# Top-16 searches run as two interleaved chains, and the index decode in two passes instead of three

## The chip, the cores and the metric

The kernel runs on one core of a Trainium2 chip. The metric is the device time of one execution in microseconds (us). A core has these engines, each with its own in-order instruction queue: TensorE (PE in the profile; PEld is its weight loads), VectorE (DVE), ScalarE (ACT), GpSimd (POOL) and SyncE (SP, here only issuing transfers). They meet at semaphores.

## The reference

One step of a hybrid decoder layer for 256 prompt tokens and 8 sample tokens (264 columns, `T`). What matters here is the PEER block: for every token and each of 8 heads, two score vectors of 128 keys are searched for their 16 largest, the 16x16 sums are searched again, and the winners name 16 of 16384 experts.

```python
s1 = jnp.einsum('thd,hkd->thk', q[:, :, 0], keys1)
s2 = jnp.einsum('thd,hkd->thk', q[:, :, 1], keys2)
t1, i1 = lax.top_k(s1, 16)
t2, i2 = lax.top_k(s2, 16)
cand = t1[..., :, None] + t2[..., None, :]          # 16 x 16 per head
cand_idx = i1[..., :, None] * 128 + i2[..., None, :]
top, pos = lax.top_k(cand.reshape(..., 256), 16)
idx = jnp.take_along_axis(cand_idx, pos, axis=-1)
gate = jax.nn.softmax(top, axis=-1)
hid = gelu(einsum('td,thkd->thk', x, u_tab[idx]))
out = einsum('thk,thkd->td', gate * hid, v_tab[idx])
```

## The kernel before

All matrix products are made in three (or, paired, two) passes over a weight split into a high and a low part. For each half of a 128-column weight block (1 MB block, halves of 128x1024) ScalarE writes the high part, `whi` (line 165, a cast), and VectorE writes the low part, `wlo` (line 166, a subtraction). `split_w` does it as soon as a buffer pair is free; there are 4 pairs, 5 from the PEER stage on. So VectorE stands in every half of every matrix product of the program: the PE cannot enter the `wlo` products of a half before line 166 has run for it.

The program is written out in one stream by hand. `pair_block` and `col_block` write the products of one half and then call `tick(budget)`. A tick lets background generators (`tasks`) write some of their instructions between this half and the next: each `yield c` of a generator takes c from the tick's budget of 1.1, and `yield ("w", n)` sleeps n ticks. The constants in the yields thus set how many background instructions stand between two `wlo` rows of VectorE's queue. A burst of them with no yield stands there whole.

The stretch in question:

- The query projection (`col_block` over `w_q`) and then the U stage: 128 blocks `pair_block(x1_p, u_evac(e), 1.1)`, which compute x times all experts' u rows densely. In each half 8 steps of one 416-column product (line 303) and one 208-column product (line 304), 16 steps in a block; the evacuation is one `as` copy on ScalarE (line 1452), one `as` addition on VectorE (line 1453), and a Gelu every second block (1456).
- Beside it, background work. `head_topk(h)` makes the scores of a head on the PE (`scr`, `scp`) and searches them with `topk` (lines 1111 to 1116): five VectorE operations, each needing the one ahead. The processor's form of `max_index` and `match_replace` is two instructions each, MATCH_VALUE_LOAD and FIND_INDEX8 or MATCH_REPLACE8.
- `select(t, sel)`: for t = 0 and 2 a grid of 128 tokens with 8 heads, for t = 1 a small one (64 rows, 1 head). It adds the candidates (`cand`, 112 per head), searches each head's (lines 1174 to 1178), works out the two slot numbers a and b of each winner from its position (nine small steps, 1183 to 1193), and decodes them into key indices: for each quarter of the heads and each side s, `big` = (a equals slot) (1205), times `idf`, the key indices as floats (1208), summed over slots (1210). Then the softmax, `sel`.
- `select_all` runs the grids in the order 0, 1, 2. Grid 0's result is transposed by the PE (`slt`, line 1240) into `slot`, and starts `gates`, which every three ticks makes one-hot tiles `o` of four tokens on POOL (line 1289, three of four; the fourth on VectorE) and ScalarE (1290), and multiplies them on the PE (`gps`, line 1302). Grid 1 starts `sparse_experts`, which fetches expert rows `ug` by indirect transfers that POOL issues (1313) and works on them on VectorE (1383). Grid 2 runs beside both.
- `iot` holds the numbers 0 to 127 in each partition; it is fetched by POOL's queue at the program's start.

Of the kernel before, what the change touches and what calls it, by code (L numbers as in the profile page):

```python
# [31 lines left out]
TOPK = 16  # L32
# [3 lines left out]
NEG = -3.0e38  # L36
# [16 lines left out]
def hybrid_step(ctx: ExitStack, tc: tile.TileContext, xT, pT, w_in, w_dt, w_bs, w_bc, w_o, w_q, w_pg, w_pp,  # L53
                uT, vP, uR, vR, keysT, par, hpar, hist, h0, eye, tri, iota, fold, yT, o_hp, o_hs, o_cp, o_cs, o_sp, o_ss):
    nc = tc.nc
    te, ve, ac, gp, sy = nc.tensor, nc.vector, nc.scalar, nc.gpsimd, nc.sync

    cpool = ctx.enter_context(tc.tile_pool(name="cpool", bufs=1))
# [53 lines left out]
    def bank(name):  # L112
        return BG["pool"].tile([128, 512], F, name=name, tag="bg", bufs=BG["n"])
# [979 lines left out]
    def load_keys(h):  # L1093
        k = t2.tile([128, 2, 128], F, name="keys", tag="keys", bufs=2)
        gp.dma_start(out=k, in_=keysT[:, 2 * h:2 * h + 2, :])
        keys_sb[h] = k
# [10 lines left out]
            defer(3, late)  # L1107
        return f

    def topk(v, a, i, n):  # L1110
        ve.max(a[:, 0:8], v)
        ve.max_index(i[:, 0:8], a[:, 0:8], v)
        w = t2.tile([128, 128], F, name="sw", tag="sw", bufs=2)
        ve.match_replace(w[:n], a[:, 0:8], v, NEG)
        ve.max(a[:, 8:16], w[:n])
        ve.max_index(i[:, 8:16], a[:, 8:16], w[:n])

    def head_topk(h):
        load_keys(h)
        yield ("w", 2)  # L1120
        for s in range(2):
            ac.copy(zq[:, s, h, 8 * h:8 * h + 8], Q[2 * h + s][:, PT:T])
        yield ("w", 1)
        k = keys_sb.pop(h)
        ps2 = {}
        for t in (0, 2):
            t0, n, _ = TT[t]
            ps = bank("scr")
            for s in range(2):
                te.matmul(ps[:n, s * 128:(s + 1) * 128], Q[2 * h + s][:, t0:t0 + n], k[:, s], start=True, stop=True)  # L1130
            v = t2.tile([128, 2, 128], F, name="sv", tag="sv", bufs=3)
            ac.copy(v[:n].rearrange("p s k -> p (s k)"), ps[:n, 0:256])
            ps2[t] = v
            yield 0.1
        if h == 0:
            SC["ps"] = bank("scp")
        for s in range(2):
            te.matmul(SC["ps"][:64, s * 128:(s + 1) * 128], zq[:, s, h], k[:, s],
                      start=(h == 0 and s == 0), stop=(h == PH - 1), skip_group_check=True)
        if h == PH - 1:  # L1140
            v = t2.tile([128, 2, 128], F, name="sv", tag="sv", bufs=3)
            ac.copy(v[:64].rearrange("p s k -> p (s k)"), SC.pop("ps")[:64, 0:256])
            ps2[1] = v
        for t, v in sorted(ps2.items()):
            n = TT[t][1]
            for s in range(2):
                hh = h if t != 1 else 0
                topk(v[:n, s], TV[t][s][:n, hh], TI[t][s][:n, hh], n)
                yield 1.1
        Q.pop(2 * h)  # L1150
        Q.pop(2 * h + 1)
        DONE[h] = True

    def select(t, sel):

        _, n, nh = TT[t]
        sp = P["sp"]
        w = nh * TOPK
        top = sp.tile([128, nh, TOPK], F, name="top", tag="top", bufs=1)
        pos_u = sp.tile([128, nh, TOPK], U32, name="posu", tag="posu", bufs=1)  # L1160

        cand = sp.tile([128, nh, 112], F, name="cand", tag="cand", bufs=1)
        v1, v2 = TV[t][0][:n], TV[t][1][:n]
        ve.tensor_tensor(cand[:n, :, 0:64].rearrange("p h (a b) -> p h a b", b=16),
                         v1[:, :, 0:4, None].to_broadcast([n, nh, 4, 16]),
                         v2[:, :, None, :].to_broadcast([n, nh, 4, 16]), OP.add)
        ve.tensor_tensor(cand[:n, :, 64:112].rearrange("p h (a b) -> p h a b", b=4),
                         v1[:, :, 4:16, None].to_broadcast([n, nh, 12, 4]),
                         v2[:, :, None, 0:4].to_broadcast([n, nh, 12, 4]), OP.add)
        yield 1.1  # L1170
        for h in range(nh):
            cf = cand[:n, h]
            a, i = top[:n, h], pos_u[:n, h]
            ve.max(a[:, 0:8], cf)
            ve.max_index(i[:, 0:8], a[:, 0:8], cf)
            ve.match_replace(cf, a[:, 0:8], cf, NEG)
            ve.max(a[:, 8:16], cf)
            ve.max_index(i[:, 8:16], a[:, 8:16], cf)
# [3 lines left out]
        sh = sp.tile([128, w], U32, name="sh", tag="sh", bufs=2)
        ve.tensor_scalar(sh[:n], pu, 4, None, OP.logical_shift_right)
        ve.tensor_copy(ab_f[:n, 2], sh[:n])
        sh = sp.tile([128, w], U32, name="sh", tag="sh", bufs=2)
        ve.tensor_scalar(sh[:n], pu, 2, None, OP.logical_shift_right)
        ve.tensor_copy(ab_f[:n, 3], sh[:n])
        fa, fb = ab_f[:n, 0], ab_f[:n, 1]
        ve.scalar_tensor_tensor(fa, ab_f[:n, 3], -12.0, ab_f[:n, 2], OP.add, OP.max)
        ve.tensor_scalar(ab_f[:n, 2], fa, 4.0, 48.0, OP.mult, OP.add)  # L1190
        ve.scalar_tensor_tensor(ab_f[:n, 2], fa, 16.0, ab_f[:n, 2], OP.mult, OP.min)
        ve.tensor_copy(fb, pu)
        ve.tensor_tensor(fb, fb, ab_f[:n, 2], OP.subtract)
        yield 1.4
        HH = max(1, nh // 4)
        for s in range(2):
            af = ab_f[:, s].rearrange("p (h k) -> p h k", h=nh)
            idf = sp.tile([128, nh, TOPK], F, name="idf", tag="idf", bufs=1)
            ve.tensor_copy(idf[:n], TI[t][s][:n])
            sv = sel[:n, s].rearrange("p (h k) -> p h k", h=nh)  # L1200
            for h0_ in range(0, nh, HH):
                hs = slice(h0_, h0_ + HH)
                big = sp.tile([128, HH, TOPK, TOPK], F, name="big", tag="big", bufs=1)
                sh4 = [n, HH, TOPK, TOPK]
                ve.tensor_tensor(big[:n], af[:n, hs, :, None].to_broadcast(sh4),
                                 iot[:n, None, None, 0:TOPK].to_broadcast(sh4), OP.is_equal)
                yield 0.6 if nh > 1 else 0.4
                ve.tensor_tensor(big[:n], big[:n], idf[:n, hs, None, :].to_broadcast(sh4), OP.mult)
                yield 0.6 if nh > 1 else 0.4
                ve.tensor_reduce(sv[:, hs], big[:n], AX.X, OP.add)  # L1210
                yield 0.6 if nh > 1 else 0.4
        gt = sel[:n, 2].rearrange("p (h k) -> p h k", h=nh)
        ve.tensor_tensor(gt, top[:n], top[:n, :, 0:1].to_broadcast([n, nh, TOPK]), OP.subtract)
        yield ("w", 1)
        ac.activation(gt, gt, AF.Exp)
        sm = sp.tile([128, nh], F, name="sm", tag="sm", bufs=2)
        ve.tensor_reduce(sm[:n], gt, AX.X, OP.add)
        ve.reciprocal(sm[:n], sm[:n])
        ve.tensor_tensor(gt, gt, sm[:n, :, None].to_broadcast([n, nh, TOPK]), OP.mult)
        yield 0.8  # L1220
# [554 lines left out]
```

## Time and profile before

| what | value |
|---|---|
| runs shown | 2433.89, 2436.02, 2436.13 us, median 2436.02 |
| profiled execution | 2436.66 us, of which the span of the records is 2434.7 us |
| PE busy | 2410.7 us, 99% of the span |
| DVE busy | 2004.6 us, 82% |
| ACT busy | 1451.3 us, 60% |
| POOL busy | 664.9 us, 27% |
| DMA | 685.49 MB, mean 282 GB/s |

A table by stretches of time has, for each engine, the time it was busy and in brackets the number of instructions, then the granted PE clock (1.00 is full speed), the share of time that the DMA engines were busy, and GB/s. A line of the timeline has start, duration, engine, source line, operation, output<-inputs, shape, count, and in square brackets the idle time ahead of it and what ended it. A line of the waits has who waited for whom, the sum in us, how often, and the longest.

Line numbers from about 118 on move by a few lines in the changed kernel (166 becomes 167, 1453 becomes 1459).

### The profile page before, as it was taken

To read this page: it belongs to the slowest core of one execution; us is meant where nothing else is said; L and a number is where in the kernel's file an instruction comes from. 1 tells how busy PE (TensorE), PEld (TensorE's weight loads), DVE (VectorE), ACT (ScalarE), POOL (GpSimd) and SP (SyncE) were. 2 spreads that over 40 slices of the span, in tenths; PEclk is the share of its full clock that TensorE was granted. 3 is DMA by queue.
4 is the path that set the end of the run, shared out by engine and by line. 5 is a ranking of instruction groups with operands and counts; after the bars stand their busy time and mean duration, and the time that the engine had idled before them with its cause. 6 is when DMAs were issued, how large, how long until landed. Compare 5 with 4: busy or idle time off the path is not lost.

```text
span 2434.7 us, 47923 instructions
## 1 busy us (share of the span) xinstructions
PE 2410.7 (99%) x19049; PEld 2397.1 (98%) x19049; DVE 2004.6 (82%) x3178; ACT 1451.3 (60%) x2310; POOL 664.9 (27%) x716
## 2 busy tenths in 40 slices
PE   9999999999999999999999999999999999999999
PEld 9999999999999999999999999999999999999999
DVE  7788887567455578999989877789999999999997
ACT  6776664554444455754677878777554455444574
POOL 2232221000000010100149767663433233322210
PEclk9999999999999999999999999999999999999999
DMA  6697786555555555566779999999999999999553
GB/s 246 230 293 256 257 262 213 195 189 199 199 192 193 198 198 191 197 224 199 237 266 367 388 354 358 353 383 404 392 397 389 395 387 389 393 374 370 201 200 131
DMA packets 135632, 685.49 MB, mean 282 GB/s; under 512 B 15552, under 2 KB 51952, under 8 KB 61808
## 3 DMA queue, kind: packets, MB, share of 16 engines
q1 hardware_dynamic: 89168, 495.46, 56.8%
q0 software_dynamic: 28368, 156.99, 16.6%
q10 hardware_dynamic: 17872, 29.99, 3.4%
q8 instruction: 149, 2.44, 0.4%
q14 instruction: 75, 0.61, 0.1%
HBM read 644.61 MB, written 37.76 MB: 280 GB/s over the span
## 4 chain that ended last, share of the span: by engine, by line
PE 82%; DVE 11%; issue 2%; ACT 2%; DMA 2%; POOL 0%; ACTq 0%; DVEq 0%; SPq 0%; POOLq 0%
PE mm L303 21%; PE mm L264 14%; PE mm L266 14%; PE mm L265 14%; PE mm L304 11%; DVE wlo L166 5%; PE kept L303 2%; PE mm L306 1%; PE gps L1302 1%; PE kept L304 1%; ACT whi L165 1%; DMA a_d<-as 1%; DVE as L1453 1%; DMA ug<-vR,sidx 0%; DVE ug L1383 0%
## 5 line engine op out<-in xcount | busy, mean ns | idle before, releaser
L166 DVE TENSOR_TENSOR wlo<-w,whi 128x1024 fp32r<-128x1024 f32 x916 | 1112.6, 1224 | 282.9 <-ACT whi L165 274.2
L165 ACT CAST whi<-w 128x1024 fp32r<-128x1024 f32 x916 | 953.0, 1045 | 538.1 <-PE mm L265 192.7
L303 PE MATMUL mm<-x,whi 128*128 128x416 f32 x1920 | 571.5, 365 | 0.0
L264 PE MATMUL mm<-x,whi 128*128 128x264 f32 x1920 | 532.4, 277 | 0.0
L266 PE MATMUL mm<-x,wlo 128*128 128x264 f32 x1920 | 530.2, 276 | 1.1 <-DVE wlo L166 1.1
L265 PE MATMUL mm<-x,whi 128*128 128x264 f32 x1920 | 529.9, 276 | 0.0
L304 PE MATMUL mm<-x,wlo 128*128 128x208 f32 x2048 | 502.7, 256 | 7.8 <-DVE wlo L166 7.8
L303 PE MATMUL mm<-co,whi 128*128 128x416 f32 x1680 | 490.5, 361 | 0.0
L304 PE MATMUL mm<-co,wlo 128*128 128x208 f32 x1792 | 436.9, 254 | 0.0
L304 PEld LDWEIGHTS mm<-x,wlo 128*128 128x128 f32 x2048 | 393.2, 193 | 11.0 <-DVE wlo L166 10.9
L303 PEld LDWEIGHTS mm<-x,whi 128*128 128x128 f32 x1920 | 365.8, 191 | 1.2 <-issue 0.5
L266 PEld LDWEIGHTS mm<-x,wlo 128*128 128x128 f32 x1920 | 362.9, 189 | 1.7 <-DVE wlo L166 1.7
L264 PEld LDWEIGHTS mm<-x,whi 128*128 128x128 f32 x1920 | 362.9, 189 | 1.4 <-issue 1.4
L265 PEld LDWEIGHTS mm<-x,whi 128*128 128x128 f32 x1920 | 362.9, 189 | 0.0
L304 PEld LDWEIGHTS mm<-co,wlo 128*128 128x128 f32 x1792 | 341.9, 192 | 0.0
L303 PEld LDWEIGHTS mm<-co,whi 128*128 128x128 f32 x1680 | 317.9, 189 | 0.0
L1289 POOL TENSOR_SCALAR o<-iot,slot,slot 128x128 f32<-128x128 f32 x156 | 232.0, 1494 | 2.1 <-issue 0.4
L1313 POOL DMA_INDIRECT ug<-vR,sidx x56 | 114.2, 2039 | 258.9 <-DVE x1s L1393 222.6
L1313 POOL DMA_INDIRECT ug<-uR,sidx x56 | 94.1, 1680 | 210.3 <-DVE ug L1383 186.9
L1383 DVE SCALAR_TENSOR_TENSOR ug<-ug,x1s 128x2048 f32<-128x2048 f32 x56 | 128.0, 2285 | 11.6 <-DMA ug<-uR,sidx 11.5
L1393 DVE SCALAR_TENSOR_TENSOR x1s<-ug,scf,x1s 128x2048 f32<-128x2048 f32 x53 | 124.3, 2346 | 12.5 <-DMA ug<-vR,sidx 12.5
L906 POOL CAST r1h<-r1gbh 128x2 fp32r<-128x2 f32 x16 | 7.5, 469 | 439.8 <-DVE mxl L251 439.8
(402 smaller groups left out, 4136.1 us busy)
## 6 DMA issues: line engine op xcount, KB each, us to landing
w<-uT SPq DMA_DIRECT2D x128, 1024.0 KB
w<-vP SPq DMA_DIRECT2D x128, 1024.0 KB
w<-w_in SPq DMA_DIRECT2D x118, 1024.0 KB
w<-w_bc SPq DMA_DIRECT2D x16, 1024.0 KB
w<-w_bs SPq DMA_DIRECT2D x16, 1024.0 KB
w<-w_o SPq DMA_DIRECT2D x16, 1024.0 KB
w<-w_q SPq DMA_DIRECT2D x16, 1024.0 KB
w<-w_pg SPq DMA_DIRECT2D x16, 1024.0 KB
```

Source lines behind the costliest of these rows:

```text
L165: ac.copy(hi, w)
L166: ve.tensor_tensor(lo, w, hi.bitcast(F), OP.subtract)
L264: te.matmul(ps, wh, vh, start=(first and q == 0), stop=False)
L265: te.matmul(ps, wh, vl, start=False, stop=False)
L266: te.matmul(ps, wl, vh, start=False, stop=(last and q == n - 1))
L303: te.matmul(ps, hi[:, ws], both, start=(first and kb == 0), stop=False)
L304: te.matmul(ps[:, :TD], lo[:, ws], one, start=False, stop=False)
L306: te.matmul(ps, hi[:, ws], both, start=False, stop=last)
L1289: (gp if q < 3 else ve).tensor_scalar(o1[:, q], iot, slot[0][:, c], slot[2][:, c], OP.is_equal, OP.mult)
L1313: gp.indirect_dma_start(out=t, out_offset=None, in_=tab, in_offset=bass.IndirectOffsetOnAxis(ap=sidx[:, c:c + 1], axis=0))
L1383: ve.scalar_tensor_tensor(t, t, 1.0, x1s, OP.mult, OP.mult, accum_out=shid[:, c:c + 1])
L1393: ve.scalar_tensor_tensor(x1s, t, scf[:, c:c + 1], x1s, OP.mult, OP.add)
```

## The change

Three edits, all in `topk` and `select`.

1. `topk` and the five search lines of `select` become one generator, `top16(chains, cost)`, which works two chains in turn: max of the first, max of the second, index of the first, index of the second, and so on. In `head_topk` the two chains are the two sides s of a head; in `select` two heads. A yield stands ahead of the second chain's `match_replace` and one at the end. In `head_topk` both cost 1.1 (before: 1.1 after each side). In `select` they cost 0.95 for grid 0 and 1.2 for grids 1 and 2 (before: 0.95 after each head).
2. The decode: `far` (new, 16 numbers 0, 256, 512, ... in each partition) is added to the key indices, once for each side. Then `big` = index + 256 * slot - 256 * a, and the smallest magnitude over the slots is the index of slot a. So each quarter takes two passes where there were three, two quarters are worked in turn, and `big` has two buffers.
3. The small steps stand in another order, with one more yield among them (1.1, then 1.5, where there was one of 1.4). `far` is written by POOL at the program's start, from `iot`.

```diff
+    far = cpool.tile([128, TOPK], F, name="far")
...
     gp.dma_start(out=iot, in_=iota)
+    gp.tensor_scalar(far, iot[:, 0:TOPK], 256.0, None, OP.mult)
...
-    def topk(v, a, i, n):
-        ve.max(a[:, 0:8], v)
-        ve.max_index(i[:, 0:8], a[:, 0:8], v)
-        w = t2.tile([128, 128], F, name="sw", tag="sw", bufs=2)
-        ve.match_replace(w[:n], a[:, 0:8], v, NEG)
-        ve.max(a[:, 8:16], w[:n])
-        ve.max_index(i[:, 8:16], a[:, 8:16], w[:n])
+    def top16(chains, cost):
+
+        for v, a, i, w in chains:
+            ve.max(a[:, 0:8], v)
+        for v, a, i, w in chains:
+            ve.max_index(i[:, 0:8], a[:, 0:8], v)
+        for k, (v, a, i, w) in enumerate(chains):
+            if k:
+                yield cost
+            ve.match_replace(w, a[:, 0:8], v, NEG)
+        for v, a, i, w in chains:
+            ve.max(a[:, 8:16], w)
+        for v, a, i, w in chains:
+            ve.max_index(i[:, 8:16], a[:, 8:16], w)
+        yield cost
...
-        for h in range(nh):
...
-            yield 0.95
+        for h in range(0, nh, 2):
+            yield from top16([(cand[:n, q], top[:n, q], pos_u[:n, q], cand[:n, q]) for q in range(h, min(h + 2, nh))],
+                             1.2 if t else 0.95)
...
+        for q in range(2):
+            ve.tensor_scalar(sh[q][:n], pu, 4 - 2 * q, None, OP.logical_shift_right)
+        ve.tensor_copy(fb, pu)
+        for q in range(2):
+            ve.tensor_copy(ab_f[:n, 2 + q], sh[q][:n])
+        yield 1.1
         ve.scalar_tensor_tensor(fa, ab_f[:n, 3], -12.0, ab_f[:n, 2], OP.add, OP.max)
...
+        ve.tensor_tensor(idf[0][:n], TI[t][0][:n], far[:n, None, :].to_broadcast([n, nh, TOPK]), OP.add)
         ve.tensor_tensor(fb, fb, ab_f[:n, 2], OP.subtract)
-        yield 1.4
+        ve.tensor_tensor(idf[1][:n], TI[t][1][:n], far[:n, None, :].to_broadcast([n, nh, TOPK]), OP.add)
+        ve.tensor_scalar(ab_f[:n, 0:2], ab_f[:n, 0:2], 256.0, None, OP.mult)
+        yield 1.5
...
-                ve.tensor_tensor(big[:n], af[:n, hs, :, None].to_broadcast(sh4),
-                                 iot[:n, None, None, 0:TOPK].to_broadcast(sh4), OP.is_equal)
-                yield 0.6 if nh > 1 else 0.4
-                ve.tensor_tensor(big[:n], big[:n], idf[:n, hs, None, :].to_broadcast(sh4), OP.mult)
-                yield 0.6 if nh > 1 else 0.4
-                ve.tensor_reduce(sv[:, hs], big[:n], AX.X, OP.add)
+                ve.tensor_tensor(big[:n], idf[s][:n, hs, None, :].to_broadcast(sh4),
+                                 af[:n, hs, :, None].to_broadcast(sh4), OP.subtract)
+                bigs.append(big)
+                yield 0.65 if nh > 1 else 0.4
+            for (s, hs), big in zip(todo[k:k + 2], bigs):
...
+                ve.tensor_reduce(sv[:, hs], big[:n], AX.X, OP.min, apply_absolute_value=True)
                 yield 0.6 if nh > 1 else 0.4
```

How VectorE's queue stands at three places. In square brackets are the semaphores that an instruction waits for; `DVE_49` is VectorE's own, so such a row waits for an earlier VectorE instruction to be complete.

First, VectorE in the search of the first head (`tv`, `ti`: values and indices found; `sv`: scores; `sw`: scores with the first eight struck out). Before:

```order
L1111 MAX tv_11869<-sv 128x8 [waits Activation_49]
L1112 MAX_INDEX ti_11875<-tv_11869,sv 128x8 [waits DVE_49]
L1114 MATCH_REPLACE sw<-tv_11869,sv 128x128
L1115 MAX tv_11869<-sw 128x8 [waits DVE_49]
L1116 MAX_INDEX ti_11875<-tv_11869,sw 128x8 [waits DVE_49]
L166 TENSOR_TENSOR wlo_100<-w_95,whi_96 128x1024 [waits PE_49,Activation_49]
```

After:

```order
L1115 MAX tv_11871<-sv 128x8 [waits Activation_49]
L1115 MAX tv_11872<-sv 128x8
L1117 MAX_INDEX ti_11877<-tv_11871,sv 128x8 [waits DVE_49]
L1117 MAX_INDEX ti_11878<-tv_11872,sv 128x8 [waits DVE_49]
L1121 MATCH_REPLACE sw<-tv_11871,sv 128x128
L167 TENSOR_TENSOR wlo_101<-w_96,whi_97 128x1024 [waits PE_49,Activation_49]
L1121 MATCH_REPLACE sw<-tv_11872,sv 128x128
L1123 MAX tv_11871<-sw 128x8 [waits DVE_49]
L1123 MAX tv_11872<-sw 128x8 [waits DVE_49]
L1125 MAX_INDEX ti_11877<-tv_11871,sw 128x8 [waits DVE_49]
L1125 MAX_INDEX ti_11878<-tv_11872,sw 128x8 [waits DVE_49]
```

The instructions are the same; a row that waits for VectorE has another chain's row between it and the one it waits for, and the `wlo` rows stay at one a chain.

Second, VectorE at the end of grid 0's search and its small steps (`posu`: positions of the winners, `sh` and `abf`: the slot numbers in the making). Before, between two `wlo` rows:

```order
L1177 MAX top<-cand 128x8 [waits DVE_49]
L1178 MAX_INDEX posu<-top,cand 128x8 [waits DVE_49]
L1183 TENSOR_SCALAR sh<-posu 128x128 [waits DVE_49]
L1184 CAST abf<-sh 128x128 [waits DVE_49]
L1186 TENSOR_SCALAR sh<-posu 128x128
L1187 CAST abf<-sh 128x128 [waits DVE_49]
L1189 SCALAR_TENSOR_TENSOR abf<-abf 128x128 [waits DVE_49]
L1190 TENSOR_SCALAR abf<-abf 128x128 [waits DVE_49]
L1191 SCALAR_TENSOR_TENSOR abf<-abf 128x128 [waits DVE_49]
L1192 CAST abf<-posu 128x128
L1193 TENSOR_TENSOR abf<-abf 128x128 [waits DVE_49]
L166 TENSOR_TENSOR wlo_103<-w_13079,whi_99 128x1024 [waits DMAHW7_49,Activation_49]
```

After:

```order
L1188 TENSOR_SCALAR sh<-posu 128x128 [waits DVE_49]
L1188 TENSOR_SCALAR sh<-posu 128x128
L1189 CAST abf<-posu 128x128
L1191 CAST abf<-sh 128x128 [waits DVE_49] x2
L167 TENSOR_TENSOR wlo_104<-w_13082,whi_100 128x1024 [waits DMAHW7_49,Activation_49]
L1193 SCALAR_TENSOR_TENSOR abf<-abf 128x128 [waits DVE_49]
L1194 TENSOR_SCALAR abf<-abf 128x128 [waits DVE_49]
L1195 SCALAR_TENSOR_TENSOR abf<-abf 128x128 [waits DVE_49]
L1197 TENSOR_TENSOR idf<-ti_11877,far 128x128
L1198 TENSOR_TENSOR abf<-abf 128x128 [waits DVE_49]
L1199 TENSOR_TENSOR idf<-ti_11878,far 128x128
L1200 TENSOR_SCALAR abf<-abf 128x256 [waits DVE_49]
```

A `wlo` row now stands among the small steps, and the two `idf` rows have moved up among them.

Third, VectorE in the decode of grid 0. Before:

```order
L1205 TENSOR_TENSOR big<-abf,iot 128x512
L1208 TENSOR_TENSOR big<-big,idf 128x512 [waits DVE_49]
L166 TENSOR_TENSOR wlo_102<-w_93,whi_97 128x1024 [waits DMAHW0_49,Activation_49]
L1210 TENSOR_REDUCE sel_13934<-big 128x32 [waits DVE_49]
L1205 TENSOR_TENSOR big<-abf,iot 128x512 [waits DVE_49]
```

After:

```order
L1210 TENSOR_TENSOR big<-idf,abf 128x512 [waits DVE_49]
L1210 TENSOR_TENSOR big<-idf,abf 128x512
L167 TENSOR_TENSOR wlo_101<-w_94,whi_97 128x1024 [waits PE_49,Activation_49]
L1459 TENSOR_TENSOR as<-mm,as 128x208 [waits Activation_49]
L1216 TENSOR_REDUCE sel_13936<-big 128x32 [waits DVE_49] x2
```

The middle pass is gone, and two quarters stand side by side. Counted in halves of products, the `slt` transposes of grid 0 stand three halves earlier in the PE's queue, those of grid 2 six halves earlier.

More of the change, by code (lines that the diff above doesn't have):

```diff
@@ L1145, in head_topk @@
             n = TT[t][1]
[L1146 to L1149, printed above, removed]
+            hh = h if t != 1 else 0
+            ws = [t2.tile([128, 128], F, name="sw", tag="sw", bufs=2) for s in range(2)]
+            yield from top16([(v[:n, s], TV[t][s][:n, hh], TI[t][s][:n, hh], ws[s][:n]) for s in range(2)], 1.1)
         Q.pop(2 * h)
@@ L1170, in select @@
         yield 1.1
-        for h in range(nh):
[L1172 to L1178, printed above, removed]
-            yield 0.95
+        for h in range(0, nh, 2):
+            yield from top16([(cand[:n, q], top[:n, q], pos_u[:n, q], cand[:n, q]) for q in range(h, min(h + 2, nh))],
+                             1.2 if t else 0.95)
         pu = pos_u[:n].rearrange("p h k -> p (h k)")
         ab_f = sp.tile([128, 4, w], F, name="abf", tag="abf", bufs=1)
[L1182 to L1187, printed above, removed]
-        fa, fb = ab_f[:n, 0], ab_f[:n, 1]
+        sh = [sp.tile([128, w], U32, name="sh", tag="sh", bufs=2) for _ in range(2)]
+        fa, fb = ab_f[:n, 0], ab_f[:n, 1]
+        for q in range(2):
[4 more added lines that the diff above has]
+        yield 1.1
         ve.scalar_tensor_tensor(fa, ab_f[:n, 3], -12.0, ab_f[:n, 2], OP.add, OP.max)
@@ L1191, in select @@
         ve.scalar_tensor_tensor(ab_f[:n, 2], fa, 16.0, ab_f[:n, 2], OP.mult, OP.min)
-        ve.tensor_copy(fb, pu)
+        idf = [sp.tile([128, nh, TOPK], F, name="idf", tag="idf", bufs=2) for _ in range(2)]
+        ve.tensor_tensor(idf[0][:n], TI[t][0][:n], far[:n, None, :].to_broadcast([n, nh, TOPK]), OP.add)
         ve.tensor_tensor(fb, fb, ab_f[:n, 2], OP.subtract)
-        yield 1.4
+        ve.tensor_tensor(idf[1][:n], TI[t][1][:n], far[:n, None, :].to_broadcast([n, nh, TOPK]), OP.add)
@@ L1195, in select @@
+        ve.tensor_scalar(ab_f[:n, 0:2], ab_f[:n, 0:2], 256.0, None, OP.mult)
+        yield 1.5
         HH = max(1, nh // 4)
[L1196 to L1205, printed above, removed]
-                                 iot[:n, None, None, 0:TOPK].to_broadcast(sh4), OP.is_equal)
-                yield 0.6 if nh > 1 else 0.4
-                ve.tensor_tensor(big[:n], big[:n], idf[:n, hs, None, :].to_broadcast(sh4), OP.mult)
-                yield 0.6 if nh > 1 else 0.4
-                ve.tensor_reduce(sv[:, hs], big[:n], AX.X, OP.add)
+        sh4 = [n, HH, TOPK, TOPK]
@@ new lines, in select @@
+        todo = [(s, slice(h0_, h0_ + HH)) for s in range(2) for h0_ in range(0, nh, HH)]
+        for k in range(0, len(todo), 2):
+            bigs = []
+            for s, hs in todo[k:k + 2]:
+                af = ab_f[:, s].rearrange("p (h k) -> p h k", h=nh)
+                big = sp.tile([128, HH, TOPK, TOPK], F, name="big", tag="big", bufs=2)
+                ve.tensor_tensor(big[:n], idf[s][:n, hs, None, :].to_broadcast(sh4),
[3 more added lines that the diff above has]
+            for (s, hs), big in zip(todo[k:k + 2], bigs):
+                sv = sel[:n, s].rearrange("p (h k) -> p h k", h=nh)
+                ve.tensor_reduce(sv[:, hs], big[:n], AX.X, OP.min, apply_absolute_value=True)
```

## The prediction

> **What bounds the kernel now.** I read the page's chain first, then the waits of the PE, then busy times by stretch, then VectorE's timeline there.
>
> ```profile
> PE 82%; DVE 11%; issue 2%; ACT 2%; DMA 2%; POOL 0%; ACTq 0%; DVEq 0%; SPq 0%; POOLq 0%
> ```
>
> The chain is the PE's, with 11% (about 268 us) on VectorE. That 11% is not what a faster VectorE would give: where two engines run neck and neck, the chain hops between them. The stretches tell more:
>
> ```profile
> 1056.00:1132.00 76.00, 76.00 (x533) 74.54 (x532) 73.12 (x245) 41.12 (x71) 1.62 (x3) 1.00 0.66 218
> 1132.00:1160.00 28.00, 23.70 (x155) 21.80 (x154) 26.66 (x89) 14.62 (x21) 0.00 (x0) 1.00 0.64 211
> 1160.00:1197.00 37.00, 35.03 (x233) 34.71 (x233) 36.55 (x56) 18.23 (x25) 0.18 (x1) 0.95 0.69 225
> 1220.00:1247.00 27.00, 24.54 (x176) 24.01 (x175) 25.08 (x82) 23.37 (x45) 11.72 (x13) 0.98 0.71 251
> ```
>
> The first busy column is the PE, the third VectorE. In 1056 to 1132 (searches of the heads) the PE is never idle though VectorE is 96% busy. In grid 0's search (1132 to 1160), its decode (to 1197) and grid 2's search (1220 to 1247) the PE idles 4.3, 2.0 and 2.5 us. All waits of the PE between 1130 and 1350:
>
> ```profile
> PE mm L304 <- DVE wlo L166: 6.7, 8, 2.8
> PE gps L1302 <- POOL o L1289: 2.7, 3, 1.4
> PE slt L1240 <- DVE sel L1219: 2.0, 1, 2.0
> PE x1t L1343 <- ACT x1s L1333: 0.6, 1, 0.6
> ```
>
> That is 12.0 us. After the three longest gaps the granted PE clock (the column ahead of the last two) falls:
>
> ```profile
> 1160.00:1166.00 6.00, 6.00 (x32) 5.93 (x32) 5.93 (x10) 0.00 (x0) 0.00 (x0) 0.72 0.50 178
> 1246.00:1250.00 4.00, 4.00 (x19) 3.93 (x18) 3.97 (x8) 2.19 (x4) 0.00 (x0) 0.57 0.51 174
> 1324.00:1328.00 4.00, 3.65 (x15) 3.60 (x16) 4.00 (x5) 1.92 (x3) 3.79 (x4) 0.59 0.50 180
> ```
>
> 6 x 0.28 = 1.7, 4 x 0.43 = 1.7, 4 x 0.41 = 1.6: together 5.0 us. So the PE loses 17.0 us in the whole stretch that the change touches, and that, with little more, is all it can win.
>
> Is the PE really at its pace in the searches of the heads?
>
> ```profile
> 1101.53 0.36 PE L303 MATMUL mm<-x,whi 128*128 128x416 f32 x1
> ...
> 1105.27 0.36 PE L303 MATMUL mm<-x,whi 128*128 128x416 f32 x1
> ```
> ```profile
> L304 PE MATMUL mm<-x,wlo 128*128 128x208 f32 x236 | 57.5, 254 | 0.0
> L1130 PE MATMUL scr<-keys,np 128*128 128x128 f32 x40 | 5.3, 275 | 0.0
> L1138 PE MATMUL scp<-keys,zq 128*64 128x128 f32 x20 | 3.3, 285 | 0.0
> ```
> ```profile
> 1452.97 1.08 PE L1302 MATMUL gps<-o,o 128*128 128x128 f32 x8
> 1453.80 0.42 PE L303 MATMUL mm<-x,whi 128*128 128x416 f32 x1
> ```
>
> Thirteen steps in 3.74 us are 0.288 each, so 2.30 us for a half of eight; small products take 0.83 / 8 = 0.104 each. The 236 steps and 60 small products of 1056 to 1132 are 68.0 + 6.2 = 74.2 us of 76: at most 1.8 us to win there.
>
> **The change part by part.** *The searches.* One old chain, and the `wlo` behind it:
>
> ```profile
> 1136.86 0.27 DVE L1178 FIND_INDEX8 posu<-top,cand 128x8 uint32<-128x112 f32 x1
> 1137.04 0.26 DVE L1174 MAX8 top<-cand 128x8 f32<-128x112 f32 x1
> 1137.34 0.09 DVE L1175 MATCH_VALUE_LOAD posu<-top,cand 128x8 f32 x1
> 1137.41 0.27 DVE L1175 FIND_INDEX8 posu<-top,cand 128x8 uint32<-128x112 f32 x1
> 1137.72 0.09 DVE L1176 MATCH_VALUE_LOAD cand<-top,cand 128x8 f32 x1
> ...
> 1138.66 1.21 DVE L166 TENSOR_TENSOR wlo<-w,whi 128x1024 fp32r<-128x1024 f32 x1
> 1139.79 0.27 DVE L1174 MAX8 top<-cand 128x8 f32<-128x112 f32 x1
> ```
>
> Read the starts. The MAX8 of the next head, which waits for nothing, starts 0.18 after the FIND_INDEX8 ahead of it, inside its duration; a step that needs the one ahead starts 0.30 to 0.31 after it. Each of a chain's four dependences costs about 0.12, and the chain takes 1.62. Two chains in turn leave every dependence covered by the other chain's step: 1.62 - 4 x 0.12 = 1.14 a chain. (VectorE's self-waits stay; what they wait for is done by then.) A `wlo` occupies 1.13.
>
> In VectorE time per half of products: before, `wlo` 1.13, `as` 0.29 in every second half (rows below), and at 0.95 a head against a budget of 1.1 some 8/7 heads, 1.85: 3.13 against the PE's 2.30. Seven halves, 5.8 us too slow. After: 4 pairs over the same 7.6 of budget, 9.1 us over 7 halves, 1.30 each: 2.58, 1.9 us too slow in all. VectorE may be ahead by four halves (five buffer pairs), 9 us, so the 1.9 is hidden by the lead with which grid 0 begins. That lead is what the old head searches had eaten: their chains have 1.59 us (MAX8 to the `wlo` behind it) against
>
> ```profile
> 1033.99 0.29 DVE L1111 MAX8 tv<-sv 128x8 f32<-128x128 f32 x1
> ...
> 1035.58 1.21 DVE L166 TENSOR_TENSOR wlo<-w,whi 128x1024 fp32r<-128x1024 f32 x1
> ```
>
> 1.59 - 3 x 0.12 = 1.23 now, since only three of their steps wait: 1.13 + 0.15 + 1.59 = 2.87 a half before, 2.51 after, against the PE's 74.2 / 29.5 = 2.51. The lead no longer shrinks. For grid 2 the PE's half is 2.30 + 0.83/3 = 2.58 with `gps` every third half; VectorE's is 3.2 before, and at cost 1.2 a half pair (9.6 of budget, 8.7 halves) 1.28 + 1.05 + 0.1 = 2.4 after: faster than the PE.
>
> *The small steps.*
>
> ```profile
> 1153.02 1.21 DVE L166 TENSOR_TENSOR wlo<-w,whi 128x1024 fp32r<-128x1024 f32 x1
> ...
> 1156.17 0.23 DVE L1183 TENSOR_SCALAR sh<-posu 128x128 uint32<-128x128 uint32 x1
> ...
> 1158.36 2.35 DVE L166 TENSOR_TENSOR wlo<-w,whi 128x1024 fp32r<-128x1024 f32 x2
> ```
>
> A head's search and nine steps stand between two `wlo`: 5.3 us, more than two halves; this is the 2.8 us wait of line 304, and the clock falls behind it. The new yield puts a `wlo` among them. Three more instructions (two `idf` sums for two casts, one scaling) cost what the better order saves; I count this zero, between -1 and +1 us, hidden by the lead.
>
> *The decode.*
>
> ```profile
> 1180.84 0.37 DVE L1453 TENSOR_TENSOR as<-mm,as 128x208 f32<-128x208 f32 x1
> 1181.13 0.68 DVE L1205 TENSOR_TENSOR big<-abf,iot 128x512 f32<-128x512 f32 x1
> 1181.84 0.69 DVE L1208 TENSOR_TENSOR big<-big,idf 128x512 f32<-128x512 f32 x1
> 1182.45 1.22 DVE L166 TENSOR_TENSOR wlo<-w,whi 128x1024 fp32r<-128x1024 f32 x1
> ```
>
> A pass occupies 0.61, or 0.71 if the next needs it. A big grid has 24 before, some 15.8 us, and 16 after, 9.8. The new subtraction and the smallest-magnitude reduction have no row: bounds are 0.61 (same shapes) and twice that, if a magnitude costs a second pass; I take 0.61, the nearest. Per half: 1.28 + 1.1/0.625 x 0.61 = 2.35, where 2.46 stood, against 2.30.
>
> *`far`.* POOL now waits for `iot` early in its queue, ahead of the `pad` rows:
>
> ```profile
> 21.60 0.29 POOL L429 TENSOR_SCALAR after<-tri 128x128 f32<-128x128 f32 x1 [5.06 <-DMA tri<-tri]
> ...
> 27.16 1.41 POOL L529 COPY ncp<-pad 128x3 f32<-128x3 f32 x1 [4.69 <-ACT pad L521]
> ```
>
> `tri` lands at 21.6, `iot` was issued 0.55 us behind it, and POOL then idles 4.69 us: nothing, unless `iot` came 5 us later.
>
> *What moves.* Grid 0's `slt`, the gates and the expert rows stand three halves earlier, with POOL's transfers; the last gates were at PE pace already, so this costs nothing unless POOL falls behind.
>
> The sum: line 304's waits 6.7, all gone; `slt` 2.0, of which 1.5 (VectorE must be about two halves ahead there); POOL's 2.7, half of it, 1.4: POOL's fetches queue behind VectorE's late rows, but not only; two dips of the clock 3.4, and half of the third, 0.8. 13.8 us. From the profiled execution's 2436.66 that is 2422.9; this execution is 0.6 us above the median, less than the runs' spread of 2.2. I forecast 2423.
>
> **The rivals.** *Order buys nothing (13%).* If a pair of chains takes 3.24 as before, only the burst is split and the decode shortened. Then of 17.0 us the first `wlo` waits outside the burst (1.5 + 0.5), `slt` 2.0, x1t 0.6, POOL 2.7 and the third dip 1.6 stay, 8.9: 2428.5. Against it: the start 0.18 behind an unfinished instruction. The Trainium skill, "VectorE: DVE Perf Modes", section "The DRAIN you can't avoid", says that the next operation starts only when the pipe is empty, and its rules that only the number of operations counts; that speaks against this change, and would give this rival. The trace here disagrees, 0.18 against 0.30, as the page itself allows in its later section on instructions with no wait between them.
>
> *All of it (10%).* POOL's waits go too, and the head searches give their 1.8: 17.0 + 1.8, 2418.
>
> *The loss moves on (12%).* The PE now asks for gates sooner, or the new passes take 1.2 us (2.35 becomes 3.4 a half), and 9 to 17 us of stalls return: 2432 to 2440, same.
>
> *Slower (5%): POOL.*
>
> ```profile
> 1254.15 2.84 POOL L1289 TENSOR_SCALAR o<-iot,slot,slot 128x128 f32<-128x128 f32 x3
> 1285.07 8.01 POOL L1289 TENSOR_SCALAR o<-iot,slot,slot 128x128 f32<-128x128 f32 x3
> ```
>
> Three `o` take 2.84 us alone and 8.0 beside a busy VectorE. With 1.35 us of fetches per three halves that is 9.4 against the PE's 7.7. `o` is made six halves (15.5 us) ahead; from about 10 slow groups in a row it stalls the PE, and with 22 the loss is 1.6 x 22 - 15.5 = 20 plus dips: 2443. Against it: the passes with two tensors are halved, and slow groups now come four at a time.
>
> **How the numbers follow.** 60% for the forecast; its own range is 2419 (all 17.0 us go) to 2428 (5 of the 13.8 us stay). 80% range: 2417.5, just under "all", to 2432, which leaves out most of the last two rivals. A measurement here can tell 0.2%, 4.9 us: faster is under 2431.1. Forecast, "all" and most of "order" make 0.80; same 0.15; slower 0.05.
>
> **What would show it.** In the changed profile: index searches that start about 0.2 after the MAX8 ahead; pairs of about 2.3 us; no wait of line 304 over 1 us between 1130 and 1250, the clock at 1.00 there; 16 big passes a grid at 0.61; heads' searches at an unchanged PE pace. I am wrong if the waits on `wlo` stay, or if those on POOL's `o` grow by as much.

## The result, and the profile after

| kernel | median, us | runs |
|---|---|---|
| before | 2436.07 | 6 (2433.89 to 2442.15) |
| changed | 2420.47 | 6 (2417.90 to 2421.56) |

The ratio is 0.9932 with a 95% interval of 0.9919 to 0.9944: 0.7% faster, beyond the 0.2% that the prediction set as the least that can be told, where 2423.0 (2417.5 to 2432) was forecast. The profiled execution took 2419.28 us, its span is 2417.1, 17.6 less than the span before; by the medians the gain is 15.6. Of all the runs below one execution stands apart, 6280.23 us of the kernel with the heads' searches alone in turn, and its ratio leaves it out.

First the page's chain of the changed kernel, the engines' shares:

```profile
PE 94%; DVE 2%; DMA 2%; issue 1%; ACT 1%; POOL 0%; ACTq 0%; SPq 0%; DVEq 0%; POOLq 0%
```

VectorE's share of the chain fell from 11% to 2%. The same four stretches of time as before, same columns (PE, its weight loads, VectorE, ScalarE, POOL, then the granted clock):

```profile
1056.00:1132.00 76.00, 76.00 (x533) 74.54 (x532) 70.93 (x249) 44.13 (x75) 1.61 (x3) 1.00 0.69 231
1132.00:1160.00 28.00, 28.00 (x197) 28.00 (x197) 27.69 (x98) 15.78 (x23) 0.00 (x0) 1.00 0.71 236
1160.00:1197.00 37.00, 37.00 (x261) 37.00 (x261) 33.94 (x70) 26.08 (x43) 13.00 (x13) 1.00 0.73 246
1220.00:1247.00 27.00, 27.00 (x195) 27.00 (x194) 26.88 (x62) 21.68 (x40) 9.85 (x7) 1.00 0.84 295
```

The PE is busy throughout, at clock 1.00. In 28 us of grid 0's search it now gets 197 instructions done where it did 155. In the heads' searches ahead of it the count is 533 in both kernels, so the PE had nothing to win there. The profile has no wait of the PE between 1130 and 1350, where the four rows of before stood.

Now VectorE's timeline in the changed kernel: a pair of grid 0's heads, from the first MAX8 to the `wlo` behind it, and then the small steps between two `wlo`:

```profile
1132.50 0.45 DVE L1115 MAX8 top<-cand 128x8 f32<-128x112 f32 x2
1132.86 0.07 DVE L1117 MATCH_VALUE_LOAD posu<-top,cand 128x8 f32 x1
1132.92 0.27 DVE L1117 FIND_INDEX8 posu<-top,cand 128x8 uint32<-128x112 f32 x1
1133.10 0.07 DVE L1117 MATCH_VALUE_LOAD posu<-top,cand 128x8 f32 x1
...
1134.67 1.21 DVE L167 TENSOR_TENSOR wlo<-w,whi 128x1024 fp32r<-128x1024 f32 x1
...
1148.95 0.36 DVE L1188 TENSOR_SCALAR sh<-posu 128x128 uint32<-128x128 uint32 x2
...
1149.64 1.22 DVE L167 TENSOR_TENSOR wlo<-w,whi 128x1024 fp32r<-128x1024 f32 x1
1150.77 0.29 DVE L1193 SCALAR_TENSOR_TENSOR abf<-abf 128x128 f32<-128x128 f32 x1
...
1152.37 1.22 DVE L167 TENSOR_TENSOR wlo<-w,whi 128x1024 fp32r<-128x1024 f32 x1
```

The two MAX8 start 0.18 apart, and the value load of the first index search starts 0.36 behind the first of them, so 0.18 behind the second, where a dependent step stood 0.30 behind the one ahead. The pair takes 1134.67 - 1132.50 = 2.17 us; two chains took 3.24. The twelve small steps take 0.69 + 1.60 = 2.29 us, where nine took 1158.36 - 1156.17 = 2.19: near the zero that was forecast.

The decode's passes, which had no row before, start 0.60 apart, as the 0.61 taken for them; the reduction by magnitude is no longer than the subtraction:

```profile
1161.89 0.68 DVE L1210 TENSOR_TENSOR big<-idf,abf 128x512 f32<-128x512 f32 x1
1162.49 0.68 DVE L1216 TENSOR_REDUCE sel<-big 128x32 f32<-128x512 f32 x1
1163.09 1.22 DVE L167 TENSOR_TENSOR wlo<-w,whi 128x1024 fp32r<-128x1024 f32 x1
```

So far this is the forecast. Two things in the profile are not. The products of the U stage (input `x`) and of the V stage behind it (input `co`), one row each, give first and last start; before, then after:

```profile
L303 PE MATMUL mm<-x,whi x1920: 339/362/694, 1053.1 to 1722.4; 128*128 128x416 f32 x192
L303 PE MATMUL mm<-co,whi x1680: 339/362/487, 1723.0 to 2324.2; 128*128 128x416 f32 x187
```
```profile
L304 PE MATMUL mm<-x,whi x1920: 339/362/443, 1054.2 to 1701.7; 128*128 128x416 f32 x192
L304 PE MATMUL mm<-co,whi x1680: 339/362/487, 1702.3 to 2306.3; 128*128 128x416 f32 x187
```

The U stage went from 669.3 to 647.5, 21.8 us shorter: more than the 17.0 that I had called all it could lose, with little more. But it begins 1.1 us later, and the V stage, which the diff does not touch, went from 601.2 to 604.0, 2.8 us longer. With 0.3 in the rest, 21.8 - 1.1 - 2.8 - 0.3 = 17.6. Three questions follow: which edit brings the 21.8, what costs the 1.1, and what the 2.8.

### The profile page after: what moved, and what is told of

The parts are those of the page before. It is cut to its first block, busy times and chain, and to the rows that moved or that the text cites. A ratio compares the mean times of both kernels' runs of the same rounds, so it can differ in the third digit from the quotient of the medians.

```text
span 2417.1 us, 47908 instructions
## 1 busy us (share of the span) xinstructions
PE 2402.7 (99%) x19049; PEld 2392.0 (99%) x19049; DVE 1978.4 (82%) x3163; ACT 1453.0 (60%) x2310; POOL 646.8 (27%) x717
## 4 chain that ended last, share of the span: by engine, by line
PE 94%; DVE 2%; DMA 2%; issue 1%; ACT 1%; POOL 0%; ACTq 0%; SPq 0%; DVEq 0%; POOLq 0%
PE mm L304 27%; PE mm L265 15%; PE mm L267 15%; PE mm L266 14%; PE mm L305 13%; PE kept L304 2%; PE gps L1308 2%; PE mm L307 2%; DVE wlo L167 1%; PE kept L305 1%; DMA al<-a_d 1%; DMA ug<-vR,sidx 0%; PE yS L1360 0%; DMA w<-w_in 0%; DVE x1s L1399 0%
## 5 line engine op out<-in xcount | busy, mean ns | idle before, releaser
L1295 POOL TENSOR_SCALAR o<-iot,slot,slot 128x128 f32<-128x128 f32 x156 | 217.4, 1399 | 1.8
```

The lines of the kernel that those rows point to most:

```text
L1295: (gp if q < 3 else ve).tensor_scalar(o1[:, q], iot, slot[0][:, c], slot[2][:, c], OP.is_equal, OP.mult)
```

## The experiments

Theory A: VectorE's time between `wlo` rows was too long, in the heads' searches (where it only eats the lead) and in grid 0's, and the order shortens it. The rivals stand with each run. The kernel before ran beside each group of runs; its medians there are 2435.16 to 2436.07, so medians of different groups can be compared to about 1 us, and ratios are to the kernel before of the same group.

**The changed kernel with each chain worked to its end.** In `top16`, instructions, yields and costs unchanged:

```diff
-        for v, a, i, w in chains:
-            ve.max(a[:, 0:8], v)
-        for v, a, i, w in chains:
-            ve.max_index(i[:, 0:8], a[:, 0:8], v)
         for k, (v, a, i, w) in enumerate(chains):
             if k:
                 yield cost
+            ve.max(a[:, 0:8], v)
+            ve.max_index(i[:, 0:8], a[:, 0:8], v)
             ve.match_replace(w, a[:, 0:8], v, NEG)
-        for v, a, i, w in chains:
             ve.max(a[:, 8:16], w)
...
```

> The changed kernel with every chain worked to its end before the next one starts; instructions, yields and costs as in the changed kernel. Theory A (the dependence of 0.12 us is paid where a chain's steps follow one another, and VectorE then loses its lead over the PE in the head searches and in grid 0's search): a pair of chains takes 3.2 us again, pairs of 3.2 against 2.2 mean that waits of the PE on wlo come back between 1132 and 1160 (2 to 4 us, with one dip of the clock of 1.7) and slt's wait of 1 to 2 us; time 2424 to 2430, about 2427. Rival B (only the count of instructions and the split burst matter, the order buys nothing): 2420 to 2421, as the changed kernel, and no wait on wlo.

Measured: 2433.79 us, ratio to before 0.9991 (0.9982 to 1.0). Two chains take 3.25 us again (MAX8 at 1136.23, `wlo` at 1139.48). The PE's waits in this kernel between 1050 and 1360:

```profile
PE mm L305 <- DVE wlo L167: 3.0, 7, 1.3
PE slt L1242 <- DVE sel L1221: 2.8, 1, 2.8
PE gps L1304 <- POOL o L1291: 1.7, 2, 0.9
```

Rival B falls: without the order, nearly all of the gain is gone. But the time is above A's 2430 too: by the ratio the two-pass decode and the split burst together are worth some 2 us (0 to 4), not the 8 that I gave them.

**The kernel before with the heads' searches alone in turn.**

```diff
-            for s in range(2):
-                hh = h if t != 1 else 0
-                topk(v[:n, s], TV[t][s][:n, hh], TI[t][s][:n, hh], n)
-                yield 1.1
+            hh = h if t != 1 else 0
+            ws = [...]
+            yield from top16([(v[:n, s], ..., ws[s][:n]) for s in range(2)], 1.1)
```

> The kernel before with the heads' searches alone in two chains in turn; grids' searches, small steps and decode as before. Theory A: the PE was never idle in the heads' searches, so nothing is won there, but VectorE enters grid 0's search with its lead of up to four halves (9 us) where it had 1.5 halves; the first waits on wlo (1.5 us between 1132 and 1150) go and part of the burst's 2.8 us, with a dip of the clock; grid 2's waits stay. Time 2429 to 2433, about 2431. Rival B (the order buys nothing): 2436. Rival C (the lead does not matter, only what stands between two wlo rows does): the burst's wait stays at 2.8 us and the time is 2435 to 2436.

Measured: 2432.20, ratio 0.9981 (0.9972 to 0.9990). The lead does what A says: between 1132 and 1160 the PE is busy 26.27 us where it was 23.70. The longest wait on `wlo` falls from 2.8 to 1.7, so rival C falls with B. Yet of the 5.7 us by which it is ahead where the kernel before stands at 1166, and 4.1 at 1279 (starts of the blocks' last products, counted from the first block's), 1.4 are left at the stage's end. Its waits after 1400 have one that before did not have:

```profile
PE gps L1309 <- POOL o L1296: 3.5, 1, 3.5
```

**The kernel before with the two-pass decode alone** (`far`, `idf` with `far`, one subtraction and one reduction a quarter; one yield of 0.6 ahead of them).

> The kernel before with the two-pass decode alone; searches and small steps in the old order. Theory A: the decode stands behind the waits on wlo of grid 0's search and the burst, so those stay (4.3 us and the dip of 1.7); the decode's own 2.0 us (slt) go and some of POOL's 2.7; time 2431 to 2434, about 2432.5. Rival B (the count of instructions is what pays, order nothing): the decode and the burst's split are the whole gain of 15.6, of which this is the larger half: 2424 to 2429.

Measured: 2432.37, ratio 0.9986 (0.9977 to 0.9994), as A has it. All of the PE's waits there are on `wlo`; `slt`'s and POOL's are gone:

```profile
PE mm L305 <- DVE wlo L167: 8.2, 9, 2.8
```

**The kernel before with the burst split.**

```diff
         ve.tensor_copy(ab_f[:n, 3], sh[:n])
+        yield 1.1
```

> The kernel before with one yield of 1.1 put among the nine small steps. Theory A: the longest wait on wlo (2.8 us) and the dip of the clock behind it (1.7) shrink, because a wlo now stands among the steps, but VectorE is still as late in sum, so the time comes back in smaller waits: gain 2 to 5 us, 2431 to 2434. Rival C (the burst and the clock's dips behind it are most of the loss): gain 7 to 10, 2426 to 2429. Rival D (a clock dip needs a gap of over 2 us, and nothing else of the burst counts): 1.7 for each of grids 0 and 2, 2432 to 2433, with no dip left and the sum of the waits as before.

Measured: 2435.96, ratio 0.9999 (0.9990 to 1.0008): nothing, which is below every theory's figure. The 2.8 us wait is gone from the PE's waits, and others have taken its place:

```profile
PE mm L304 <- DVE wlo L166: 4.5, 10, 1.4
PE gps L1303 <- POOL o L1290: 3.8, 1, 3.8
PE slt L1241 <- DVE sel L1220: 3.5, 1, 3.5
```

11.8 us where there were 12.0, and the clock still falls behind the last two of these: the split takes no work from VectorE, so the PE waits elsewhere. Still, the U stage is 3.3 us shorter in the profile (1053.1 to 1719.1) and the V stage 5.6 longer (606.8). In the V stage stands a wait of the PE on `wlo` of 3.6 us, behind a wait of VectorE of 7.2 us on `al`: the extra 2.8 us of the changed kernel, but larger.

**The changed kernel with the heads' searches one chain at a time** (two calls of `top16` with one chain each, 1.1 after each).

> The changed kernel with the heads' searches one chain at a time (1.1 after each, as before the change); the grids' searches stay two in turn. Theory A (VectorE's time against the PE's pace, and the lead it carries): the head searches eat the lead again, the PE stands 0.9 us later at 1122 and waits on wlo in grid 0's search, some 4 us; grid 2 keeps its gain. 2423 to 2426, about 2424.5. Rival B (the lead at the start of grid 0 does not matter once its own searches are short): 2420 to 2421.

Measured: 2427.22, ratio 0.9967 (0.9955 to 0.9979): even more than A's range. The lead that the heads' searches eat is worth some 7 of the 15.6 us. But it was not lost where I said (only 0.6 us on `wlo`); the first row is the largest of its waits up to 1380:

```profile
PE slt L1247 <- DVE sel L1226: 2.8, 1, 2.8
PE gps L1309 <- POOL o L1296: 1.0, 1, 1.0
```

Up to 1154 its U blocks keep pace with the changed kernel's. They fall back 0.65 us by the waits on `wlo` and 6.0 more around the one wait on `slt`: 2.8 of waiting, and a fall of the clock behind it that costs 3.1 (last section). VectorE has no lead left at the end of the decode, and the PE pays for it there at once.

**The changed kernel without the split.**

```diff
             ve.tensor_copy(ab_f[:n, 2 + q], sh[q][:n])
-        yield 1.1
```

> The changed kernel without the new yield of 1.1 among the small steps, so that all twelve stand between two wlo rows. Theory A: the burst is now about 2.4 us of small steps beside a lead of some halves, so no wait on wlo comes back in the U stage; and the phase of the expert rows at the start of the V stage is that of before, so the 5.4 us wait of VectorE on the fetch of al and its 1.5 us of PE wait go: 2417 to 2419. Rival B (the split is what takes the 2.8 us wait and the dip away): wait and dip come back, 2423 to 2425. Rival C (the wait for al has nothing to do with this yield): 2420 to 2421.

Measured: 2417.85, ratio 0.9929 (0.9916 to 0.9942). There is no wait of the PE in the whole U stage, burst or not (nor one on `wlo` in the next kernel, which has the old burst): the 2.8 us wait was lack of lead, not lack of a `wlo` among the steps. Rival B falls. The times do not set A apart from C, the intervals overlap; the V stage does, with 601.7:

```profile
L304 PE MATMUL mm<-co,whi x1680: 339/362/487, 1701.7 to 2303.4; 128*128 128x416 f32 x187
```

VectorE still waits for `al` there, 3.8 us, but the PE's share is 0.2. So A's time came, half by another way than it said. From the last V product to the end it takes 111.8 us against the changed kernel's 110.8; why, is open.

**The kernel before with the order alone** (`top16` in heads and grids with the costs of the change; old small steps, old decode, no `far`).

> The kernel before with the searches of heads and grids two chains in turn, and nothing else of the change: old small steps in one burst, old three-pass decode. Theory A (order is most of the gain, as the changed kernel with serial chains lost 13 of its 15 us): 2421 to 2425, about 2423, with slt's wait of up to 2 us and the burst's wait under 1 us. Rival B (order and decode pay only together: the gain is there only when VectorE's sum falls below the PE's in every stretch): 2427 to 2431.

Measured: 2419.99, ratio 0.9933 (0.9920 to 0.9946). This is the whole result, from the first edit alone. Its waits up to 1380, none on `wlo`:

```profile
PE gps L1303 <- POOL o L1290: 2.1, 1, 2.1
PE slt L1241 <- DVE sel L1220: 1.9, 2, 1.3
```

Its U stage takes 653.9, 6.4 longer than the changed kernel's, but it begins at 1053.0 and its V stage is 601.3. Much of the 6.4 comes at one place, the 2.1 us wait on `o` at 1332 and a fall of the clock behind it (13 PE instructions in 1332 to 1336, clock 0.57). Of what the other two edits win in the U stage, they lose 4.5 ahead of it and behind it (1.2, 2.7 and 0.6); the 1.9 that is left in the profiles does not show in the medians.

**The changed kernel with idle work on VectorE.**

```diff
             ve.match_replace(w, a[:, 0:8], v, NEG)
+            for _ in range(2):
+                ve.tensor_tensor(dump, iot, ident, OP.add)
```

> The changed kernel, chains in turn, with two additions of a 128x128 tile that nobody reads behind each chain's match_replace: some 0.5 us of VectorE a chain, about what working the chains one behind another costs. Theory A (what counts is VectorE's time between wlo rows, however it is spent): the gain of the order is gone, 2431 to 2435, with waits on wlo from 1132 on. Rival B (the order itself counts, for instance because wlo does not stand behind a chain of waits): 2420 to 2424.

Measured: 2436.74, ratio 1.0003 (0.9992 to 1.0014). A pair of additions stands 0.53 us ahead of the next row:

```profile
1134.61 0.61 DVE L1124 TENSOR_TENSOR dump<-iot,ident 128x128 f32<-128x128 f32 x2
1135.13 0.48 DVE L1126 MAX8 tv<-sw 128x8 f32<-128x128 f32 x2
```

Two pairs are 1.06 us for two chains: what the order saves in a grid (3.24 - 2.17), and 0.25 more than it saves in a head (3.16 against 2.35). With the order in place and the time given back, the gain is gone. In the profiled execution, at 2444.48 the slowest of its eleven, the U stage takes 667.6, 20.1 longer than the changed kernel's, and the PE's waits on `wlo` up to 1380 are there:

```profile
PE mm L306 <- DVE wlo L168: 5.2, 11, 1.3
```

Rival B falls: it is VectorE's time that counts, and the order acts by way of it.

**The changed kernel with `al` fetched earlier**, on one chip with the next three.

```diff
-            if k + 1 < NE // 4:
+            if k + 1 < NE // 4 and k + 1 not in AL:
                 load(k + 1)
...
                 CO[4 * k + e] = flat[:, e]
+            if k + 2 < NE // 4:
+                load(k + 2)
```

> The changed kernel with the fetches of gl and al for the block after next written behind co of this block, some two halves earlier in POOL's queue, ahead of an expert-row fetch that waits for VectorE. Theory A (the V stage is 2.8 us longer than before because al is fetched behind a waiting expert-row fetch, and VectorE waits 5.4 us for it with a wlo behind): VectorE's wait on al goes, the PE's 1.5 us of waits on wlo at the start of the V stage go, the V stage (first to last product of it with whi) is 601 to 602 us and not 604.0, the time 2417 to 2419. Rival B (POOL then waits for co and lets expert rows come late): V stage 604 or longer, 2420 or more.

Measured: 2423.50, ratio 0.9945 (0.9931 to 0.9958); the changed kernel beside it 2419.90. A falls. The wait on `al` is gone, but VectorE waits for expert rows in its place, and the V stage takes 605.3:

```profile
DVE x1s L1399 <- DMA ug<-vR,sidx: 7.2, 3, 4.4
```

**The changed kernel with `far` written just ahead of `spawn(select_all())`.**

> The changed kernel with far written by POOL just ahead of the search of grid 0 and not at the program's start. Theory A (far waits for iot at 22 us, and pad, cacc and two wlo behind it come later): the PE's waits before 62 us fall from 1.2 to 0.4, the dtr product stands at 59.3 again and not 60.2 to 60.4, the U stage begins at 1053.0 and not 1054.0; time 0.9 less than the changed kernel's beside it. Rival B (the 0.9 us come from elsewhere, for instance from the other program length): U stage at 1054, no difference.

Measured: 2419.46, ratio 0.9926 (0.9912 to 0.9939). By the trace A holds: the PE's waits between 12 and 62 us, first in the changed kernel, then here:

```profile
PE mm L267 <- DVE wlo L167: 1.2, 3, 0.5
```
```profile
PE mm L267 <- DVE wlo L167: 0.4, 1, 0.4
```

The `dtr` product stands at 59.1 and no longer at 60.4, the U stage begins at 1052.8. In the median of the runs 0.4 us of that is seen, less than their spread; this execution has a wait of 1.0 us on POOL's `o` that the changed kernel's first profile did not have.

**The changed kernel again** (on the chip of these four).

> The changed kernel once more, on the same chip as the three others: 2418 to 2421.

Measured: 2419.90, ratio 0.9931 (0.9917 to 0.9944); its profiled execution, the slowest of its five runs at 2424.53, has the PE's wait in the V stage at 3.5 us where the first had 1.5, behind the same 5.3 us wait of VectorE on `al`.

**No split, late `far`, early `al` together.**

> The changed kernel without the split of the small steps, with far written late, and with the early fetch of gl and al. Theory A: the three add: no wait of the PE on VectorE in the U stage, U stage from 1053.0, V stage 601 to 602: 2415.5 to 2417.5, about 2416.5 and 3 to 4 less than the changed kernel. Rival B (the V stage's phase is a matter of chance, and moving the fetches spoils it): V stage of 603 or more, 2418 to 2421.

Measured: 2417.63, ratio 0.9927 (0.9913 to 0.9941). No wait of the PE in the U stage, which is 647.3 long and starts at 1052.9; the V stage is 603.3, longer than without the early fetch, as the run with that fetch alone would have it. Medians of 2417.6 to 2417.9 stand here and without the split, 2419.9 to 2420.5 for the changed kernel, but the intervals overlap almost wholly: no version has been shown to be faster than the changed kernel.

## Why the prediction was right, point by point

- *An instruction that does not need the one ahead starts 0.18 behind it, one that does 0.30.* Right, and the core of the result. The chain came out at 2.17 / 2 = 1.09 and not 1.14, since value loads shrank too (0.07 where it was 0.09). The Trainium skill, "VectorE: DVE Perf Modes", section "The DRAIN you can't avoid", has the next operation start only when the pipe is empty and says that a semaphore between operations costs nothing extra; the run with serial chains contradicts both as a rule of time here, at equal numbers of instructions it is 13 us slower than the changed kernel. That section itself points to a later one on two instructions with no wait between them, for those that start earlier, and the trace agrees with that, 0.18.
- *Line 304's waits, 6.7, all gone.* Right in sum. The step behind the largest of them failed: I gave the 2.8 us to the burst and the new yield. Split alone bought nothing in the time of the whole, and unsplit with the order there was no wait. The yield moves a wait; the lead removes it.
- *The heads' searches: no loss of the PE there, but the lead shrinks.* Right, and larger than I took it to be in that run's expectation: 2427.22 with that lead taken away, so some 7 us hang on a stretch in which the PE never waits.
- *`slt` 1.5 of 2.0, POOL half of 2.7, 0.8 of the third dip.* Under-sized in the first profile, where none of them is left; further profiles of changed kernels with late `far` or run again show 1.0 us on POOL's `o`. Across the runs it is the decode that goes with the waits on `o`: over the U stage they are 2.1 to 4.9 us in the four kernels with the old three-pass decode, whatever their order, and 0 to 1.7 in nine profiles with the new one (3.6 with the idle work on VectorE). By what way is not shown. Between 1130 and 1400 POOL's queue stood behind late `ug` rows of VectorE for up to 18.9 us at a time, and now at most 5.6, but also once for 13.5 behind the PE; before, then after:

```profile
POOL ug L1313 <- DVE ug L1383: 46.1, 7, 18.9
```
```profile
POOL ug L1319 <- DVE ug L1389: 33.8, 8, 5.6
POOL ug L1319 <- PE mm L305: 13.5, 1, 13.5
```

- *After the three longest gaps the clock falls.* Misread: the falls stand behind the waits of 2.78, 1.87 and 1.41 us. The second longest, 1.97 on `slt`, has none, the clock is 1.00 behind it:

```profile
1196.00:1200.00 4.00, 4.00 (x30) 4.00 (x30) 3.15 (x7) 3.59 (x10) 3.14 (x5) 1.00 0.78 300
```

  The 5.0 us that the falls cost do not depend on this.
- *The PE loses 17.0 us, and that is the ceiling.* Mis-sized: the U stage gained 21.8. I had counted the PE's idle time, 12.0, and the clock's 5.0. Between 1132 and 1350 the rows are, before and after:

```profile
1132.00:1350.00 218.00, 206.02 (x1410) 202.25 (x1409) 202.99 (x402) 148.95 (x264) 100.43 (x74) 0.98 0.79 282
```
```profile
1132.00:1350.00 218.00, 218.00 (x1560) 217.99 (x1560) 194.17 (x401) 165.65 (x296) 121.37 (x86) 1.00 0.86 313
```

  150 instructions fewer at 218 / 1560 = 0.140 are 21.0 us. The weight loads (second pair) idle 15.75 us; with the 5.0 of the clock that is 20.8. It fits that a product whose weights could not be loaded ahead costs more than its wait; that this is the reason was not tested.
- *`far` costs nothing unless `iot` comes 5 us later.* Wrong. The step that failed is the slack: I took it from POOL's idle 4.69 us, which stands behind POOL's first `pad` copies. But ScalarE was already waiting for the first of them, 1.35 us. POOL now waits for `iot` until 22.2, and has `far` and the fills to write first that it used to write before its wait: the copy goes from 21.85 to 22.97, and ScalarE's wait becomes 2.35. Over all profiles the copy starts at 21.6 to 21.9 without the early `far` (six) and at 22.5 to 23.5 with it (eight). The rows are ScalarE's before, then ScalarE's and POOL's after:

```profile
22.09 0.54 ACT L526 ACTIVATE cacc<-pad,cpar 128x288 f32<-128x288 f32 x1 [1.35 <-POOL pad L523]
```
```profile
23.20 0.54 ACT L528 ACTIVATE cacc<-pad,cpar 128x288 f32<-128x288 f32 x1 [2.35 <-POOL pad L525]
```

```profile
22.21 0.28 POOL L423 TENSOR_SCALAR far<-iot 128x16 f32<-128x16 f32 x1 [5.40 <-DMA iot<-iota]
...
22.97 0.19 POOL L525 COPY pad<-hst 128x24 f32<-128x24 f32 x1
```

  The convolution behind it is late with it, and the PE waits on `wlo` 0.8 us more. The kernel with the late `far` gave that back.
- *What moves costs nothing.* Wrong by 2.8 us, 600 us away. In the changed kernel VectorE stands before this row, with `wlo` rows queued behind it:

```profile
1724.06 0.96 DVE L1500 TENSOR_TENSOR al<-al,gl 128x768 f32<-128x768 f32 x1 [5.40 <-DMA al<-a_d]
```

  By kernels: with the new yield the V stage takes 603.6 to 608.9 (eight profiles), without it 601.2 to 601.7 (five) and 603.3 with the early fetch. That the yield brings it is shown by the two runs that add or take it alone. By what way is open: it may move the expert rows against the `al` rows, but to fetch `al` earlier only made the expert rows late.
- *The rival "Order buys nothing", 2428.5.* Its time was wrong: serial chains give 2433.8. Its sum let waits go one by one with the edit nearest to them, where only VectorE's sum decides.

The mechanism was the one forecast, but that the size came so near is in part luck. Where 13.8 us were forecast, the U stage gave 21.8 in the profiles, 8.0 more; and 4.2 that were not foreseen were lost elsewhere (1.1, 2.8 and 0.3). That leaves 17.6, or 15.6 by the medians.

## What to carry to other kernels

Where an in-order engine feeds another just in time, add up its time over the whole stretch, and count the lead with which it arrives: a wait that is cut at one place comes back at the next unless time is taken out of the queue, and slack won where nobody waits is spent later. Two independent chains worked in turn take time out of it at equal instruction counts. Before an instruction is put into a queue or a yield into a hand-made schedule, look at what stands behind it, and at what is paired with what hundreds of us later.

## What the runs showed of the hardware

- The fall of the PE's clock after a gap is not certain. The same wait of 2.77 us on `slt` had no fall behind it in the serial kernel and one in the kernel with serial heads (10 us around the wait, 52 against 30 PE instructions, clock 1.00 against 0.66):

```profile
1180.00:1190.00 10.00, 7.23 (x52) 6.99 (x51) 8.62 (x16) 5.62 (x11) 1.21 (x3) 1.00 0.72 235
```
```profile
1180.00:1190.00 10.00, 7.23 (x30) 6.87 (x30) 7.60 (x17) 7.04 (x15) 5.37 (x7) 0.66 0.78 254
```

  22 instructions at 0.14 are 3.1 us, more than the wait. The Trainium skill, "TensorE: Matmul & The Clock Gate", section "What's actually happening", puts the half rate behind at least one idle window of about 3.4 us; here a gap of 2.77 sufficed, once of twice, and in the kernel before one of 1.87, where one of 1.97 did not. In the serial kernel the clock falls even behind two short waits on `o`, 0.76 and 0.90 us, and the PE does 28 instructions in 6 us:

```profile
1278.00:1284.00 6.00, 5.60 (x28) 5.54 (x29) 2.44 (x4) 4.41 (x10) 5.59 (x7) 0.72 0.99 404
```

  So the length of a wait alone does not tell here whether the clock falls. What else decides was not tested.
- From a value load to its index search are 0.06 us in the order of the change, and 0.07 to 0.08 where the load had to wait for the row ahead (the loads are 0.07 and 0.09 long).
- Two additions of 128x128 into the same tile, one behind the other, occupy 0.53 us, 0.61 from the first start to the last end.
